# Moving a state-space stage's step-size chain ahead of its convolutions, with a ring of three decay tiles, on one Trainium2 core

## The chip, the cores and the metric

The kernel runs on one core of a Trainium2 chip. The metric is device time in microseconds (us): the median of three runs, lower is better. TensorE (PE) does the matmuls, VectorE (DVE), ScalarE (ACT) and GpSimd (POOL) the elementwise work, SyncE (SP) issues most DMAs and ACT a few. Each engine and each issuing queue takes its instructions in a fixed order; an instruction that waits holds up all that stands behind it.

## The reference, cut to what matters

Two blocks follow each other. The first (a sliding-window attention beside a diagonal state-space layer, then a sparse attention) is untouched. The second computes, for 1024 tokens `h` of width 1024:

```python
proj = h @ w_in                       # xs, z, B, C, dt_raw, glu, cgate
xbc  = silu(conv4(concat(xs, B, C)))  # 4 taps, causal, per channel
dt   = softplus(dt_raw + dt_bias);  a = -exp(a_log)
adt  = dt * a                         # per chunk of 128 tokens:
a_cs = cumsum(adt)                    # running sums of the steps
ldec = exp(a_cs[t] - a_cs[s]), t >= s # "decay" of each head
y_diag = (C B^T * ldec) @ (xs * dt);  state = state * exp(a_cs[-1]) + B^T @ (xs*dt*exp(a_cs[-1]-a_cs))
y_off  = (C @ state) * exp(a_cs)
y_ssm  = rms((y_diag + y_off + d_skip * xs) * silu(z))
u      = glu_a * sigmoid(glu_b);  u = silu(layer_norm(conv31(u)))
y_conf = u * silu(cgate)
out    = concat(y_ssm, y_conf) @ w_out;  h = layer_norm(alpha * h + out)  # then a gated projection
```

## The kernel before, in words

All matmuls of the projections are done in three passes over split operands (a high and a low half, `mm3`, lines 148 to 150). Their weights come in pieces of 128 x 512: SP loads `wraw`, ACT writes the high half `w` (L122), POOL the low half (L123); where `k.wdve` is 2, every second piece is made by VectorE instead (L119, L120). There are 13 slots for pieces and three for raw ones.

The change lies in `phase_c`, the second block. In program order:

1. glu: gated projection, written to `d_u2`.
2. `xbc`: first the 16 columns of `dt_raw`, transposed into `dtt`; then twelve channel tiles of xs, B, C. A tile `xi` (two halves, copied from PSUM by ACT) gets its first tap on VectorE (L1516), three more (L1518), a silu on ACT, and goes to DRAM (`d_xs`, `d_bc`). The tiles `xy` that hold the result have two buffers.
3. the 31-tap convolution of u, eight channel tiles of 31 VectorE passes in PSUM (`cy`, L1258 and L1260), summed over channels in `acc`.
4. `conf_norm`: mean by a matmul over `acc` (`mu`, L1462), subtraction (L1467), squares on ACT (L1469), their sum over channels on POOL (L1471, L1473), variance by matmuls (`var`, L1477), a power on POOL (L168), a spread by matmuls (`rb`, L1482), sixteen multiplications (L1487) and eight silus (L1488).
5. `ssd`: first the step sizes and running sums (L1539 to L1583: some 28 short VectorE passes over 128 x 128, three matmuls, and a row table written to `d_cs`), then eight chunks. A chunk loads `xh`, `bct` and, for each of two groups, a decay tile `ld` of 128 x 8 x 128 (each group has one buffer), which VectorE (L1601), ACT (exp, L1603) and VectorE again (L1614) turn into the matrix of the diagonal product; POOL scales `xh` into `xd` and `xe`; PE does `cb`, `yoff`, `ydiag`, `inc`; VectorE adds up `yS` and the state `st`.
6. cgate: silu of the projection, tile by tile through the staging ring `stg` (three buffers) to `d_cg`; then sixteen tiles `cgl` of it are loaded back (two buffers of their own) and POOL multiplies `cc` by them (L1285).
7. z: the same for z, sixteen tiles of 24 matmuls, through `stg` to `d_z` (L1292, L1293).
8. the out-projection of the convolution half: `msC` (ACT L1307, POOL L1308) times pieces of `w_out`, added to the residual `rC`, written to `d_r`. Its pool stands where the normalized input `hnTC` stood.
9. the out-projection of the state-space half and the last gated projection, which the change leaves as they are.

The program is not run in this order. A scheduler of the language sets each engine's order ahead of time: it gives each engine the instruction that is first in program order among those whose operands and buffers are free in its model, with a lead for weight pieces. A tile from a ring can be written only when the tile that held its buffer before has been read. Before the change that order puts cgate and z (6 and 7) on PE while VectorE is at the convolution (3), and the out-projection (8) among the chunks of `ssd`.

Of the kernel before, what the change touches and what calls it, by code (L numbers as in the profile page):

```python
# [26 lines left out]
WDVE = (0, 0, 0, 2, 2)  # L27
# [1183 lines left out]
def phase_c(k, out, hC):  # L1211
    hnT, sR = hC
    nc, tc, ins = k.nc, k.tc, k.ins
    V, S, G, T = nc.vector, nc.scalar, nc.gpsimd, nc.tensor
    W, Wo = ins["w_in_2"][0], ins["w_out_2"][0]
# [8 lines left out]
    sng = vp.tile([P, 8], F32, name="sng")  # L1224
    stg = sR.enter_context(k.pool("c_stg", side="right"))

    def stage():
        return stg.tile([P, 512], F32, tag="s", name="stg", bufs=3)
    k.wdve = 0
    k.psum(mm=2, tp=1, sd=3, cy=2)  # L1230

# [4 lines left out]
    for j in range(4):  # L1236
        w = [k.wpiece(W, kk, [(2576 + j * 256, 256), (3600 + j * 256, 256)]) for kk in range(KT)]
        for m in range(2):
            ct = 2 * j + m
# [6 lines left out]
                V.scalar_tensor_tensor(sg, pa, cw[:, ct, 34:35], sg, op0=ALU.add, op1=ALU.mult)  # L1246
                nc.sync.dma_start(d_u2[ct * P:(ct + 1) * P, th * 512:th * 512 + 512], sg)
    with ExitStack() as cx:
        xbc(k, cx.enter_context(k.pool("c_xbc")), W, hnT, sw, dtt, d_xs, d_bc)

    acc = up.tile([P, L], F32, name="acc")
    for ct in range(8):
# [12 lines left out]
    sV.close()  # L1265

    sS, (sp,) = stack(k.pool("ssd"))
    ssd(k, sp, dtt, dtx, d_xs, d_bc, d_ys, d_cs)

    for ch in range(2):  # L1270
        w = k.wchunk(W, 4624 + ch * 512, 512)
# [8 lines left out]
    for ct in range(8):  # L1280
        for th in range(2):
            cs = slice(th * 512, th * 512 + 512)
            cg = stg.tile([P, 512], F32, tag="cg", name="cgl", bufs=2)
            nc.sync.dma_start(cg, d_cg[ct * P:(ct + 1) * P, cs])
            G.tensor_tensor(cc[:, ct, cs], cc[:, ct, cs], cg, op=ALU.mult)  # L1285
    for ch in range(2):
# [5 lines left out]
            S.activation(zt, ps, AF.Silu)  # L1292
            nc.scalar.dma_start(d_z[tt * P:(tt + 1) * P, ch * 512:ch * 512 + 512], zt)  # L1293
    sR.close()
    k.wdve = WDVE[4]

    with ExitStack() as co:
        op = co.enter_context(k.pool("c_o", side="right"))
# [189 lines left out]
        S.activation(cc[:, ct], cc[:, ct], AF.Silu, bias=cw[:, ct, 33:34], scale=cw[:, ct, 32:33])  # L1488


def xbc(k, p, W, hnT, sw, dtt, d_xs, d_bc):
    nc = k.nc
    V, S, G, T = nc.vector, nc.scalar, nc.gpsimd, nc.tensor

    w = k.wpack(W, 2560, 16)
    for th in range(2):
        ps = k.mm()
        k.form2(ps[:16], hnT, th * 512, w, KT, 0, 16)
        dr = p.tile([16, 512], F32, tag="dr", name="dr", bufs=1)
        S.activation(dr, ps[:16], AF.Copy)  # L1500
        ps = k.tp()
        for j in range(4):
            T.transpose(ps[:, j * 16:(j + 1) * 16], dr[:, j * P:(j + 1) * P], k.ident[:16, :16])
        S.activation(dtt[:, th * 4:th * 4 + 4].rearrange("p a b -> p (a b)"), ps[:, :64], AF.Copy)
    for ci, c0 in enumerate((2048, 0, 512)):
        w = k.wchunk(W, c0, 512)
        for m in range(4):
            ct = (8, 0, 4)[ci] + m
            xi = p.tile([P, 3 + L], F32, tag="xi", name="xi", bufs=2)
            V.memset(xi[:, 0:3], 0.0)  # L1510
            for th in range(2):
                ps = k.mm()
                k.form2(ps, hnT, th * 512, w, KT, m * P)
                S.activation(xi[:, 3 + th * 512:3 + th * 512 + 512], ps, AF.Copy)
            y = p.tile([P, L], F32, tag="xy", name="xy", bufs=2)
            V.tensor_scalar(y, xi[:, 0:L], sw[:, ct, 0:1], sw[:, ct, 4:5], op0=ALU.mult, op1=ALU.add)  # L1516
            for i in range(1, 4):
                V.scalar_tensor_tensor(y, xi[:, i:i + L], sw[:, ct, i:i + 1], y, op0=ALU.mult, op1=ALU.add)  # L1518
            S.activation(y, y, AF.Silu)
            if ct >= 8:  # L1520
                nc.sync.dma_start(d_bc[(ct - 8) * P:(ct - 7) * P, :], y)
            else:
                xo = p.tile([P, 8, P], F32, tag="xo", name="xo", bufs=2)
                for h in range(2):
                    ps = k.tp()
                    for i in range(4):
                        T.transpose(ps[:, i * P:(i + 1) * P], y[:, (h * 4 + i) * P:(h * 4 + i + 1) * P], k.ident)
                    S.activation(xo[:, h * 4:h * 4 + 4].rearrange("p a b -> p (a b)"), ps, AF.Copy)
                nc.sync.dma_start(d_xs[:, ct * P:(ct + 1) * P].rearrange("(j p) c -> p j c", p=P), xo)


def ssd(k, p, dtt, dtx, d_xs, d_bc, d_ys, d_cs):
    nc, ins = k.nc, k.ins
    V, S, G, T = nc.vector, nc.scalar, nc.gpsimd, nc.tensor
    f = lambda a: a.rearrange("p a b -> p (a b)")

    t = p.tile([P, 4, P], F32, tag="ld0", name="spt", bufs=1)
    a3 = lambda i: t[:, i].rearrange("p (a b) -> p a b", b=16)
    V.tensor_tensor(a3(0), dtt, dtx[:, 0].unsqueeze(1).to_broadcast([P, 8, 16]), op=ALU.add)  # L1539
    V.tensor_scalar(t[:, 1], t[:, 0], -1.0, None, op0=ALU.mult)  # L1540
# [131 lines left out]
```

## Time and profile before

| what | value |
|---|---|
| median of three runs | 2126.88 us (2124.61 to 2127.88) |
| the profiled execution | 2116.4 us, span 2114.6 us |
| busy: PE, DVE, ACT, POOL | 91%, 73%, 38%, 41% of the span |
| POOL L123, low halves of weights | x230, 310.3 us |
| DVE L1260, the 31 taps | x232, 298.7 us, mean 1287 ns |
| granted TensorE clock, mean | 0.96 |

A busy share is an average over stages with different limits. The granted clock is a share of full speed (2.4 GHz; 0.5 is 1.2 GHz). The ends of matmuls are modelled, so a matmul's duration is longer than the distance from its start to the next one's.

### The profile page before, as it was taken

To read this page: it belongs to the slowest core of one execution; us is meant where nothing else is said; L and a number is where in the kernel's file an instruction comes from. 1 tells how busy PE (TensorE), PEld (TensorE's weight loads), DVE (VectorE), ACT (ScalarE), POOL (GpSimd) and SP (SyncE) were. 2 spreads that over 40 slices of the span, in tenths; PEclk is the share of its full clock that TensorE was granted. 3 is DMA by queue.
4 is the path that set the end of the run, shared out by engine and by line. 5 is a ranking of instruction groups with operands and counts; after the bars stand their busy time and mean duration, and the time that the engine had idled before them with its cause. 6 is when DMAs were issued, how large, how long until landed. Compare 5 with 4: busy or idle time off the path is not lost. (4 is left out here: it accounts for less than half of the span.)

```text
span 2114.6 us, 27500 instructions
## 1 busy us (share of the span) xinstructions
PE 1932.8 (91%) x9291; PEld 1565.7 (74%) x9291; DVE 1546.6 (73%) x3051; ACT 813.5 (38%) x1540; POOL 867.9 (41%) x702
## 2 busy tenths in 40 slices
PE   7988889989999898799987999999999659999998
PEld 6777777777888786677865788788888537778786
DVE  8365513674469999698879399899997488957737
ACT  5222327564456885355543121133322411144210
POOL 5566416545322233365545131222232576643204
PEclk9988989999999999899999999999999869999999
DMA  6543332313212212554444132222433445574442
GB/s 199 156 125 94 114 130 83 118 46 110 81 61 70 70 46 79 171 193 140 130 145 173 61 114 71 70 90 90 129 104 101 159 146 169 170 254 165 155 165 100
DMA packets 166694, 256.19 MB, mean 121 GB/s; under 512 B 29078, under 2 KB 77548, under 8 KB 166554
## 3 DMA queue, kind: packets, MB, share of 16 engines
q1 hardware_dynamic: 156330, 236.62, 34.9%
q10 hardware_dynamic: 10224, 17.82, 2.3%
q8 instruction: 73, 1.20, 0.2%
q14 instruction: 67, 0.55, 0.1%
HBM read 185.35 MB, written 75.06 MB: 123 GB/s over the span
## 5 line engine op out<-in xcount | busy, mean ns | idle before, releaser
L123 POOL TENSOR_TENSOR w<-wraw,w 128x512 fp32r<-128x512 f32 (+1 forms) x230 | 310.3, 1365 | 683.4 <-ACT w L122 672.1
L1260 DVE SCALAR_TENSOR_TENSOR cy<-u,cw,cy 128x1024 f32<-128x1024 f32 x232 | 298.7, 1287 | 5.7
L122 ACT ACTIVATE w<-wraw 128x512 fp32r<-128x512 f32 (+1 forms) x230 | 142.0, 622 | 196.2 <-DMA wraw<-in_w_in_dram 53.3
L149 PE MATMUL mm<-hnTC,w 128*128 128x512 f32 (+1 forms) x336 | 131.6, 392 | 0.0
L150 PE MATMUL mm<-hnTC,w 128*128 128x512 f32 (+1 forms) x336 | 131.5, 391 | 0.0
L148 PE MATMUL mm<-hnTC,w 128*128 128x512 f32 (+1 forms) x336 | 131.5, 391 | 0.0
L148 PE MATMUL mm<-w,ms 128*128 128x512 f32 x256 | 103.9, 406 | 8.8 <-ACT ms L1003 7.9
L1149 POOL TENSOR_TENSOR lgB<-lgB,sc 128x1024 f32<-128x1024 f32 (+5 forms) x48 | 84.1, 1780 | 66.9 <-DMA lgB<-d_T 53.4
L150 PE MATMUL mm<-w,ms 128*128 128x512 f32 x256 | 104.6, 409 | 6.3 <-POOL ms L1004 4.1
L1060 ACT ACTIVATE tkj<-sc,tks 128x896 bf16<-128x896 f32 (+2 forms) x93 | 96.3, 1037 | 31.9 <-DVE tks L1056 25.6
L149 PE MATMUL mm<-w,ms 128*128 128x512 f32 x256 | 101.7, 397 | 0.0
L168 POOL TENSOR_TENSOR hr<-hm,mhalf 128x2 f32<-128x2 f32 (+2 forms) x40 | 46.1, 1154 | 115.9 <-DVE hm L398 50.8
L148 PE MATMUL mm<-w,hnTB 128*128 128x512 f32 x192 | 78.0, 407 | 7.2 <-DVE qo L402 7.2
L148 PE MATMUL mm<-w,hnTA 128*128 128x512 f32 (+1 forms) x192 | 73.0, 383 | 8.9 <-DVE qo L402 8.8
L149 PE MATMUL mm<-w,hnTB 128*128 128x512 f32 x192 | 78.0, 407 | 1.8 <-POOL w L123 1.8
L148 PE MATMUL mm<-hnTB,w 128*128 128x512 f32 (+2 forms) x208 | 78.4, 377 | 0.2 <-ACT hnTB L172 0.2
L149 PE MATMUL mm<-hnTB,w 128*128 128x512 f32 (+2 forms) x208 | 78.1, 376 | 0.0
L150 PE MATMUL mm<-hnTB,w 128*128 128x512 f32 (+2 forms) x208 | 78.1, 375 | 0.0
L150 PE MATMUL mm<-w,hnTB 128*128 128x512 f32 x192 | 78.0, 406 | 0.0
L149 PE MATMUL mm<-w,hnTA 128*128 128x512 f32 (+1 forms) x192 | 73.1, 382 | 0.2 <-POOL w L123 0.2
L150 PE MATMUL mm<-w,hnTA 128*128 128x512 f32 (+1 forms) x192 | 73.3, 382 | 0.0
L148 PEld LDWEIGHTS mm<-hnTC,w 128*128 128x128 f32 (+1 forms) x336 | 61.6, 183 | 14.5
(595 smaller groups left out, 5845.6 us busy)
## 6 DMA issues: line engine op xcount, KB each, us to landing
wraw<-in_w_in_dram SPq DMA_DIRECT2D x56, 256.0 KB
wraw<-in_od_w_in_dram SPq DMA_DIRECT2D x48, 256.0 KB
wraw<-in_ev_w_in_dram SPq DMA_DIRECT2D x32, 256.0 KB
wraw<-in_w_in_dram SPq DMA_DIRECT2D x64, 128.0 KB
wraw<-in_w_out_dram SPq DMA_DIRECT2D x32, 256.0 KB
ld<-d_cs SPq DMA_DIRECT2D x16, 512.0 KB
hr<-h SPq DMA_DIRECT2D x24, 256.0 KB
d_T<-d_row SPq DMA_DIRECT2D x8, 576.0 KB
```

The costliest lines, as they stand in the source:

```text
L122: nc.scalar.activation(t[:, 0, :o], raw[:, :o], AF.Copy)
L123: nc.gpsimd.tensor_tensor(t[:, 1, :o], raw[:, :o], t[:, 0, :o].bitcast(F32), op=ALU.subtract)
L148: mm(out, aH, bH, start=start, stop=False)
L149: mm(out, aH, bL, start=False, stop=False)
L150: mm(out, aL, bH, start=False, stop=stop)
L168: self.nc.gpsimd.tensor_tensor(out, ms, self.mhalf[:, :n], op=ALU.pow)
L1060: S.activation(self.junk(n), sc[b], AF.Sign, bias=cand[:, i:i + 1], accum_out=cnt[:, i:i + 1])
L1149: G.tensor_tensor(lg[:, :n], lg[:, :n], self.masks[b], op=ALU.add)
L1260: V.scalar_tensor_tensor(py if i < 30 else y, u[:, i:i + L], cw[:, ct, i:i + 1], py, op0=ALU.mult, op1=ALU.add)
```

## The change

- The chain of step sizes becomes a function `ssd_steps`, called in `xbc` right after `dtt` is there. Its scratch tile takes one of the two `xy` buffers; `tri`, `nacs`, `eac`, `dst`, `cdc` move to the pool `c_vec`.
- The first tap of each `xbc` tile goes from VectorE to ACT.
- The decay tiles of both groups share one ring of three. `xh`, `xd` and `xe` come in halves of 512 columns: three, two and two buffers. The last chunk makes no `xe`.
- The staging ring has four buffers, and the sixteen `cgl` tiles now come from it too, ahead of z's sixteen.
- `k.wdve` is set to 2 only after the first out-projection: its pieces are all made by ACT and POOL.

```diff
@@ phase_c
-    def stage():
-        return stg.tile([P, 512], F32, tag="s", name="stg", bufs=3)
+    def stage(name="stg"):
+        return stg.tile([P, 512], F32, tag="s", name=name, bufs=4)
...
-        xbc(k, cx.enter_context(k.pool("c_xbc")), W, hnT, sw, dtt, d_xs, d_bc)
+        steps = xbc(k, cx.enter_context(k.pool("c_xbc")), vp, W, hnT, sw, dtt, dtx, d_xs, d_bc, d_cs)
...
-    ssd(k, sp, dtt, dtx, d_xs, d_bc, d_ys, d_cs)
+    ssd(k, sp, steps, dtt, dtx, d_xs, d_bc, d_ys, d_cs)
...
-            cg = stg.tile([P, 512], F32, tag="cg", name="cgl", bufs=2)
+            cg = stage("cgl")
...
     sR.close()
-    k.wdve = WDVE[4]
...
     sF.close()
+    k.wdve = WDVE[4]
@@ xbc
-        dr = p.tile([16, 512], F32, tag="dr", name="dr", bufs=1)
+        dr = p.tile([P, 512], F32, tag="xo", name="dr", bufs=2)[:16]
...
+    steps = ssd_steps(k, p, vp, dtt, dtx, d_cs)
     for ci, c0 in enumerate((2048, 0, 512)):
...
-            V.tensor_scalar(y, xi[:, 0:L], sw[:, ct, 0:1], sw[:, ct, 4:5], op0=ALU.mult, op1=ALU.add)
+            S.activation(y, xi[:, 0:L], AF.Identity, scale=sw[:, ct, 0:1], bias=sw[:, ct, 4:5])
@@ ssd_steps (the first part of ssd before)
-    t = p.tile([P, 4, P], F32, tag="ld0", name="spt", bufs=1)
+    t8 = p.tile([P, 8, P], F32, tag="xy", name="spt", bufs=2)
+    t = t8[:, 0:4]
...
-    t1 = p.tile([P, 3, P], F32, tag="ld1", name="spt1", bufs=1)
-    adt, one, ar = t1[:, 0].rearrange("p (a b) -> p a b", b=16), t1[:, 1], t1[:, 2]
+    adt, one, ar = t8[:, 4].rearrange("p (a b) -> p a b", b=16), t8[:, 5], t8[:, 6]
...
-    eac = p.tile([P, 8, 16], F32, name="eac")
+    eac = vp.tile([P, 8, 16], F32, name="eac")
...
     nc.sync.dma_start(d_cs, ar)
+    return tri, nacs, eac, dst, cdc
@@ ssd, in the loop over chunks
-        xh = p.tile([P, D], F32, tag="xh", name="xh", bufs=2)
-        nc.sync.dma_start(xh, d_xs[ts_, :])
+        xhs = []
+        for g in range(2):
+            xhs.append(p.tile([P, 512], F32, tag="xh", name="xh", bufs=3))
+            nc.sync.dma_start(xhs[g], d_xs[ts_, g * 512:(g + 1) * 512])
...
-            ld = p.tile([P, 8, P], F32, tag=f"ld{g}", name="ld", bufs=1)
+            ld = p.tile([P, 8, P], F32, tag="ld", name="ld", bufs=3)
...
-        xd = p.tile([P, D], F32, tag="xd", name="xd", bufs=1)
-        G.tensor_tensor(h3(xd), h3(xh), b64a(dtt, c), op=ALU.mult)
-        xe = p.tile([P, D], F32, tag="xe", name="xe", bufs=1)
-        G.tensor_tensor(h3(xe), h3(xd), b64a(dst, c), op=ALU.mult)
...
+        for g in range(2):
+            xd = p.tile([P, 512], F32, tag="xd", name="xd", bufs=2)
+            G.tensor_tensor(h3(xd), h3(xhs[g]), b64(dtt, g, c), op=ALU.mult)
+            xds.append(xd)
+        for g in range(2 if c < 7 else 0):
+            xe = p.tile([P, 512], F32, tag="xe", name="xe", bufs=2)
+            G.tensor_tensor(h3(xe), h3(xds[g]), b64(dst, g, c), op=ALU.mult)
+            xes.append(xe)
```

The scheduler's order moves with it. PE in `conf_norm`, before (rb spreads the reciprocal deviation; `mm<-w,hnTC` is z):

```order
L149 MATMUL mm<-w,hnTC 128x512
L150 MATMUL mm<-w,hnTC 128x512
L148 MATMUL mm<-w,hnTC 128x512
L1482 MATMUL rb_13528<-ident,rsc 128x128 x4
L1482 MATMUL rb_13529<-ident,rsc 128x128 x4
L149 MATMUL mm<-w,hnTC 128x512
L150 MATMUL mm<-w,hnTC 128x512
```

and now, from the last matmul of z's first two tiles on:

```order
L150 MATMUL mm<-w,hnTC 128x512
L1462 MATMUL mu<-acc,ones 128x512 x2
L1477 MATMUL var<-ones,acc 128x2 x8
L1482 MATMUL rb_13581<-ident,rsc 128x128 x4
L1482 MATMUL rb_13582<-ident,rsc 128x128 x4
L1619 MATMUL cb<-bct 128x128
L1620 MATMUL cb<-ident,bct 128x128
L1619 MATMUL cb<-bct 128x128
L1620 MATMUL cb<-ident,bct 128x128
L1643 MATMUL yoff<-st_13619,bct 128x512
L1648 MATMUL ydiag<-xd,ld 128x64 x8
L1655 MATMUL inc<-xe,bt 128x512
```

Before, all 384 matmuls of z stood ahead of the first chunk. Now 48 do; the next of z come after chunk 0 and the first `yoff` of chunk 1, 280 of them among chunks 1 to 7, and 56 behind the last chunk; the 384 of `msC` follow those.

ACT behind the silus of `conf_norm`, now (before, `L1603 ACTIVATE ld` met no silu of z any more):

```order
L1488 ACTIVATE cc<-cc,cw 128x1024 x8
L1616 ACT_TABLE_LOAD
L1616 ACTIVATE ld<-ld 128x1024
L1625 ACTIVATE bt<-cb 128x256
L1616 ACTIVATE ld<-ld 128x1024 x3
L1292 ACT_TABLE_LOAD
L1292 ACTIVATE stg<-mm 128x512
L1625 ACTIVATE bt<-cb 128x256
L1293 DMA d_z<-stg 128x512
```

The drain of z's first tile stands behind the fourth exp of a decay tile. Exp and silu alternate from here on: 24 table loads, where none stood among the chunks before.

SP at the end of the chunks, now (`bo` and `rC` belong to the out-projection's pool, `wraw` are its pieces):

```order
L1652 DMA d_ys<-yS 128x512 x3
L110 DMA wraw<-in_w_out_dram 128x512 x3
L187 DMA bo<-in_b_out_dram 128x1024
L1309 DMA rC<-d_h_10478 128x1024
L110 DMA wraw<-in_w_out_dram 128x512
L1309 DMA rC<-d_h_10478 128x1024 x2
L110 DMA wraw<-in_w_out_dram 128x512 x2
L1320 DMA d_r<-rC 128x512
L110 DMA wraw<-in_w_out_dram 128x512 x5
```

Five of the sixteen pieces were loaded earlier; of the eleven here eight stand behind the loads `bo` and `rC`, and the last five behind a store of the first result.

## Rows read from the trace of the kernel before

**Rows 1.** Stretches: busy us (instructions) of PE, PEld, DVE, ACT, POOL; granted clock; DMA share, GB/s.
```profile
1675.00:1709.00 34.00, 1.75 (x7) 1.16 (x6) 31.21 (x53) 11.65 (x15) 20.06 (x16) 0.55 0.59 202
1709.00:1731.00 22.00, 12.69 (x46) 9.07 (x46) 12.28 (x12) 5.02 (x8) 16.58 (x10) 0.61 0.54 181
1731.00:1885.00 154.00, 145.50 (x703) 113.44 (x702) 125.98 (x118) 29.80 (x39) 100.00 (x47) 0.98 0.54 177
1885.00:2114.60 229.60, 215.72 (x1010) 176.62 (x1008) 148.04 (x247) 60.69 (x119) 66.76 (x54) 0.99 0.45 158
```
**Rows 2.** Tile mm on PE: duration ns min/median/max, first and last start us, forms.
```profile
L150 PE MATMUL mm<-hnTC,w x336: 387/389/477, 1345.6 to 1582.5; 128*128 128x512 f32 x160, 128*16 128x512 f32 x8
...
L150 PE MATMUL mm<-w,hnTC x128: 388/389/398, 1583.1 to 1674.9; 128*128 128x512 f32 x128
L148 PE MATMUL mm<-w,msC x128: 387/389/799, 1731.3 to 1884.6; 128*128 128x512 f32 x128
```
**Rows 3.** Timeline of PE in z: start, us, line, [idle before <- releaser].
```profile
1605.13 0.39 PE L148 MATMUL mm<-w,hnTC 128*128 128x512 f32 x1
...
1605.81 0.39 PE L148 MATMUL mm<-w,hnTC 128*128 128x512 f32 x1
```
**Rows 4.** Timeline of DVE from the convolution's end to the first chunks.
```profile
1609.43 1.23 DVE L1263 TENSOR_TENSOR acc<-acc,cc 128x1024 f32<-128x1024 f32 x1
1622.51 9.65 DVE L1467 TENSOR_TENSOR cc<-cc,mu 128x512 f32<-128x512 f32 x16 [11.85 <-PE mu L1462]
...
1667.24 9.65 DVE L1487 TENSOR_TENSOR cc<-cc,rb 128x512 f32<-128x512 f32 x16 [7.29 <-PE rb L1482]
...
1709.27 0.29 DVE L1582 COPY spt<-acsT 128x128 f32<-128x128 f32 x1 [0.17 <-PE acsT L1581]
...
1729.25 2.27 DVE L1601 CUSTOM_DVE_ANT_1 ld<-ld,nacs 128x1024 f32<-128x1024 f32 x1 [1.44 <-DMA ld<-d_cs]
```
**Rows 5.** DVE by line, 1340 to 1610: busy us, mean ns | idle before <- releaser.
```profile
L1516 DVE TENSOR_SCALAR xy<-xi,sw 128x1024 f32<-128x1024 f32 x12 | 10.9, 910 | 3.3 <-ACT xi L1514 3.3
```
**Rows 6.** Tile spt (the step chain's scratch): columns as in Rows 2.
```profile
L1549 DVE TENSOR_TENSOR spt<-spt x7: 277/292/1361, 1694.3 to 1702.4; 128x128 f32<-128x128 f32 x7
```
**Rows 7.** Tile sqc (the squares) on ACT and POOL: columns as in Rows 2.
```profile
L1469 ACT ACTIVATE sqc<-cc x8: 1042/1056/1065, 1628.7 to 1650.6; 128x1024 f32<-128x1024 f32 x8
...
L1471 POOL COPY acc<-sqc x1: 1039/1039/1039, 1629.8 to 1629.8; 128x1024 f32<-128x1024 f32 x1
```
**Rows 8.** Timelines of POOL and PE at the variance.
```profile
1640.70 14.82 POOL L1473 TENSOR_TENSOR acc<-acc,sqc 128x1024 f32<-128x1024 f32 x6
1660.02 1.66 POOL L168 TENSOR_TENSOR rsc<-rsc,mhalf 128x8 f32<-128x8 f32 x1 [4.50 <-DVE rsc L1478]
...
1657.90 1.84 PE L1477 MATMUL var<-ones,acc 128*128 128x2 f32 x16
...
1666.08 1.95 PE L1482 MATMUL rb<-ident,rsc 128*128 128x128 f32 x16
```
**Rows 9.** Timeline of ACT: a table load, and a piece that waited for its load.
```profile
1663.64 1.28 ACT L1555 ACT_TABLE_LOAD   x1 [0.39 <-ACT stg L1292]
1664.93 0.21 ACT L1555 ACTIVATE ea<-dtx 128x16 f32<-128x16 f32 x1
...
1688.35 0.63 ACT L122 ACTIVATE w<-wraw 128x512 fp32r<-128x512 f32 x1 [3.82 <-DMA wraw<-in_w_out_dram]
```
**Rows 10.** Timeline of SP: issues of bo, of three pieces, and of a decay tile.
```profile
1675.34 0.33 SPq L187 DMA_DIRECT2D bo<-in_b_out_dram  x1
...
1682.83 1.37 SPq L110 DMA_DIRECT2D wraw<-in_w_out_dram  x3
...
1725.30 0.32 SPq L1600 DMA_DIRECT2D ld<-d_cs  x1
```
**Rows 11.** Tile msC on ACT and POOL: columns as in Rows 2.
```profile
L1307 ACT ACTIVATE msC<-cc x8: 1040/1048/1060, 1726.9 to 1859.8; 128x1024 fp32r<-128x1024 f32 x8
L1308 POOL TENSOR_TENSOR msC<-cc,msC x8: 2355/2652/2852, 1728.1 to 1860.9; 128x1024 fp32r<-128x1024 f32 x8
```

More of the change, by code (lines that the diff above doesn't have):

```diff
@@ L1488, in conf_norm, with xbc @@
         S.activation(cc[:, ct], cc[:, ct], AF.Silu, bias=cw[:, ct, 33:34], scale=cw[:, ct, 32:33])
-def xbc(k, p, W, hnT, sw, dtt, d_xs, d_bc):
+def xbc(k, p, vp, W, hnT, sw, dtt, dtx, d_xs, d_bc, d_cs):
     nc = k.nc
@@ L1529, in xbc, with ssd_steps @@
                 nc.sync.dma_start(d_xs[:, ct * P:(ct + 1) * P].rearrange("(j p) c -> p j c", p=P), xo)
-def ssd(k, p, dtt, dtx, d_xs, d_bc, d_ys, d_cs):
+    return steps
+def ssd_steps(k, p, vp, dtt, dtx, d_cs):
     nc, ins = k.nc, k.ins
@@ L1553, in ssd @@
     V.scalar_tensor_tensor(f(dtt), t[:, 3], 2.0, t[:, 0], op0=ALU.mult, op1=ALU.add)
-    ea = p.tile([P, 16], F32, name="ea")
+    ea = vp.tile([P, 16], F32, name="ea")
     S.activation(ea, dtx[:, 1], AF.Exp)
     V.tensor_scalar(ea, ea, -1.0, None, op0=ALU.mult)
-    t1 = p.tile([P, 3, P], F32, tag="ld1", name="spt1", bufs=1)
-    adt, one, ar = t1[:, 0].rearrange("p (a b) -> p a b", b=16), t1[:, 1], t1[:, 2]
+    adt, one, ar = t8[:, 4].rearrange("p (a b) -> p a b", b=16), t8[:, 5], t8[:, 6]
+    acs = t8[:, 7].rearrange("p (a b) -> p a b", b=16)
     V.tensor_tensor(adt, dtt, ea.unsqueeze(1).to_broadcast([P, 8, 16]), op=ALU.mult)
-    tri = p.tile([P, P], F32, name="tri")
+    tri = vp.tile([P, P], F32, name="tri")
     V.memset(tri, 1.0)
@@ L1563, in ssd @@
     V.memset(one, 1.0)
-    acs = p.tile([P, 8, 16], F32, name="acs")
-    nacs = p.tile([P, 8, 16], F32, name="nacs")
-    eac = p.tile([P, 8, 16], F32, name="eac")
-    dst = p.tile([P, 8, 16], F32, name="dst")
-    cdc = p.tile([P, 8, 16], F32, name="cdc")
+    nacs = vp.tile([P, 8, 16], F32, name="nacs")
+    eac = vp.tile([P, 8, 16], F32, name="eac")
+    dst = vp.tile([P, 8, 16], F32, name="dst")
+    cdc = vp.tile([P, 8, 16], F32, name="cdc")
     ps = k.ps("sd", "acs")
@@ L1583, in ssd @@
     nc.sync.dma_start(d_cs, ar)
+    return tri, nacs, eac, dst, cdc
+def ssd(k, p, steps, dtt, dtx, d_xs, d_bc, d_ys, d_cs):
+    nc, ins = k.nc, k.ins
+    V, S, G, T = nc.vector, nc.scalar, nc.gpsimd, nc.tensor
+    f = lambda a: a.rearrange("p a b -> p (a b)")
+    tri, nacs, eac, dst, cdc = steps
     st = [p.tile([P, 512], F32, name=f"st{g}") for g in range(2)]
@@ L1614, in ssd @@
             V.tensor_tensor(lds[g], lds[g], cb[:, g].unsqueeze(1).to_broadcast([P, 8, P]), op=ALU.mult)
-        xd = p.tile([P, D], F32, tag="xd", name="xd", bufs=1)
-        G.tensor_tensor(h3(xd), h3(xh), b64a(dtt, c), op=ALU.mult)
-        xe = p.tile([P, D], F32, tag="xe", name="xe", bufs=1)
-        G.tensor_tensor(h3(xe), h3(xd), b64a(dst, c), op=ALU.mult)
-        G.tensor_tensor(h3(xh), h3(xh), dtx[:, 2].unsqueeze(2).to_broadcast([P, 16, 64]), op=ALU.mult)
+        xds, xes = [], []
+        for g in range(2):
[6 more added lines that the diff above has]
+            xes.append(xe)
+        for g in range(2):
+            G.tensor_tensor(h3(xhs[g]), h3(xhs[g]), dtx[:, 2, g * 8:g * 8 + 8].unsqueeze(2).to_broadcast([P, 8, 64]),
+                            op=ALU.mult)
         for g in range(2):
@@ L1627, in ssd @@
             for h in range(8):
-                T.matmul(pd[:, h * 64:(h + 1) * 64], lds[g][:, h], xd[:, g * 512 + h * 64:g * 512 + (h + 1) * 64],
+                T.matmul(pd[:, h * 64:(h + 1) * 64], lds[g][:, h], xds[g][:, h * 64:(h + 1) * 64],
                          start=True, stop=True)
             V.tensor_tensor(y, pd, y, op=ALU.add)
-            G.tensor_tensor(y, y, xh[:, gs], op=ALU.add)
+            G.tensor_tensor(y, y, xhs[g], op=ALU.add)
             nc.sync.dma_start(d_ys[ts_, gs], y)
@@ L1634, in ssd @@
                 pi = k.ps("sd", "inc")
-                T.matmul(pi, bt[:, g], xe[:, gs], start=True, stop=True)
+                T.matmul(pi, bt[:, g], xes[g], start=True, stop=True)
                 V.tensor_tensor(h3(st[g]), h3(st[g]), b64(cdc, g, c), op=ALU.mult)
```

## The prediction

> **What bounds the kernel now.** I read the table of stretches first, then the matmul groups on PE, then the timelines around the point where PE stops. Up to the end of z PE is without a gap: the projections through cgate end at 1582.5 us, z at 1675 [rows 2]. Then comes a hole: in 1675 to 1709 PE is busy for 1.75 of 34 us, in 1709 to 1731 for 12.69 of 22, at a granted clock of 0.55 and 0.61 [rows 1]. From 1731 the out-projection of the convolution half runs among the chunks; PE is busy for 145.5 of 154 us and ends it at 1885.4 [rows 1, 2]. The last stage keeps PE busy for 215.7 of 229.6 us [rows 1]. So after the hole the bound is PE, and what the change can win is PE's idle time: 32 + 9 + 8.5 = about 50 us between 1675 and 1885. VectorE sets when the hole ends: it does the step chain after the last multiplication by rb, from 1676.9 to 1709.6 [rows 4].
>
> **The change part by part.** I follow PE, and ask when its queue, in the order shown for the change, reaches the last matmul of the out-projection. What stands before cgate's end is not counted: PE's matmuls there are the same, and PE now has time to spare at its end.
>
> *The convolution's end.* VectorE is the bound now up to 1610.7, the end of the last sum in acc [rows 4]. Off it go the twelve first taps, 10.9 us and up to 3.3 us of waiting before them [rows 5]; ACT has room for twelve passes of about 1.06 us [rows 7]. On it come the 28 passes of the step chain: 8 us at the median of 0.29 us, and 15 us if a quarter of them take the longest, 1.36 us [rows 6]. I take 11, since most of them lie at the median. The scratch tile holds one of two xy buffers meanwhile, so the first four tiles of xbc must each wait for the store of the one before; a couple of us of VectorE's order may be lost on that. Sum: 1610.7, with -6 to +8. The three matmuls and the DMA to d_cs move along and hide behind the taps.
>
> *conf_norm.* Before, z stood in front of mu, var and rb in PE's queue: VectorE waited 11.85 us for mu, and rb began 4.4 us after the power was done [rows 4, 8]. Now only the chain itself is left. Handing a matmul to VectorE took 1.16 us (rb at 1666.08, multiplication at 1667.24 [rows 4, 8]): 1611.9. The first two of sixteen subtractions 1.2, a square 1.06, POOL's copy 1.04 [rows 4, 7]: 1615.2. Seven sums at 14.82 / 6 = 2.47 [rows 8]: 1632.5. Variance 1.84, power 1.66, rb and its handing on 1.2, the sixteen multiplications 9.65 [rows 4, 8]: 1646.9. PE has stood still here, so I add 3 us for matmuls at half clock, the level that the hole of before shows [rows 1]: 1650, against 1676.9 before. So 27 us are won here for VectorE, and the 33 us of the step chain on top: the first chunk starts at 1650 instead of 1710.
>
> *The hole.* PE pays for both. Ahead of mu its queue now holds only 48 matmuls of z. Three of them take 0.68 us [rows 3], so they end 1582.5 + 10.9 = 1593.4, and then PE waits for VectorE: mu, var, rb and chunk 0 stand in front of the rest of z. Two things make that order: z's tiles take staging buffers behind the sixteen cgl tiles, which POOL reads only after conf_norm, and two PSUM buffers hold two tiles. From the end of the step chain to the first matmul of the next projection chunk 0 took 1731.3 - 1709.6 = 22 us [rows 2, 4]; I take it unchanged. It saves a wait for the decay table, but VectorE now does a third decay tile in it (2.27 us), and z's first drain on ACT stands behind the fourth exp, whose tile is loaded only when the first is free (3.95 us from issue to use [rows 4, 10]). So 17 to 26 us, and z goes on at 1672.
>
> *z among the chunks.* Left are 336 matmuls of z, 76.2 us [rows 3]. Chunks 1 to 7 cost PE 145.5 - 384 x 0.227 = 58.4 us in 1731 to 1885 [rows 1, 3], of which 2 are done ahead of z. With the 8.5 us of gaps of that stretch: 141 us, to 1813. VectorE has 126 us of work in that stretch [rows 1], a part of it the residual, which now goes after the chunks, so PE is the bound. For the gaps 0 to 18 us are the bounds. The ring of three, the halves of xh, xd, xe and the two that are not made save waits of VectorE and POOL that stand beside a busier PE: nothing for the end, and only the gaps if that cover were thinner.
>
> *Into the out-projection.* msC's pool stands where the input of z stood: bo was issued at 1675.34, right at z's end [rows 2, 10]. In the new order the fourth of eleven pieces is loaded behind bo and rC, and ACT makes that piece and z's last drain before the first msC. Issues 1.3 us, the load 1688.35 - 1682.83 = 5.5 us [rows 9, 10], ACT 0.6 + 0.6 + 1.05, POOL's low half 2.65 [rows 11] of which the first passes cover some: 10 us without matmuls. Then the last five pieces wait behind the first store of a result, which needs the first half tile (5.4 us): about 7 us more in the second half tile. Sum 17 (bounds 5 and 25: loads that land in 2 us, or twice as slow). That VectorE no longer makes such pieces takes work from it that was hidden, and puts it on ACT and POOL, where it is part of these 17.
>
> *Sum.* 1813 + 17 + 87.1 = 1917 for the end of the out-projection, against 1885.4: 32 us later. The last stage starts from the same state, so I leave its 229.6 us. On the profiled execution (2116.4) that is 2148; the median of the runs shown lies 10.5 us higher, so the forecast is 2126.9 + 32 = **2159 us**. All bounds on the good side (-6, -3, -5, -8.5, -12) give no change, all on the bad side (+8, +4, +10, +8) 2189.
>
> *A rule and a row.* A switch of ACT's function tables costs 1.28 us in this trace, and the next activation follows at once: load at 1663.64, exp at 1664.93 [rows 9]. Four switches in a chunk are then 5.1 us, and ACT does about 9 of 20 us (two exps of 1.06, two drains of 0.6, the copy of bt, the switches). The Trainium skill (ScalarE: Activation LUTs, What ACT_TABLE_LOAD costs) gives 1283 ns for the load, which the row bears out, and a drain of some 1380 ns on top, which it does not show. By that page's figures I estimate 14 us of ACT in a chunk, which is still no bound, so the sum would stay.
>
> **The rivals.**
> *The table switches pace the chunks (chance 0.12).* ACT's order alternates drains of z with exps, so each drain, and with it the PSUM buffer of the next tile but one, waits for a switch, and each exp for a drain. If all 24 lie on PE's path, 24 x 1.28 = 31 us: 2190 us. For it: two PSUM buffers only, and a fixed order. Against: a tile of z is 5.4 us of PE work, and a drain with its switch under 2. The same page of the Trainium skill (Rules for kernel authors) says to group functions by table set, which speaks against this order; at its 2.66 us I estimate 64 us in place of the 31.
> *Small loss (0.07).* Pieces land ahead of need and chunk 0 takes 17: 2142 us.
> *No change (0.06).* All the good bounds together, 2127.
> *Faster (0.06).* The chunks set the pace by VectorE, and PE's 58 us in them are mostly waiting: the ends of matmuls are modelled, so a busy row can hide it. Then z fits into gaps that were there anyway. It decides at 109 us for chunks 1 to 7 with z in place of 141, the point where 32 us are gone; VectorE's own work there is 126 us less the residual and the tail of chunk 0. At 100 us the run takes 2159 - 41 = 2118 us. For it: VectorE's first decay passes took 2.27 us [rows 4], and a ring of three starts them earlier. Against: z's 76 us leave only 33 for seven chunks, under 5 us each, where the rows show 8.3.
> *Forecast (0.69),* with a range of its own from 2145 to 2176.
>
> **How the numbers follow.** A median of this kernel can tell about 0.2% (4 us) from no change. Slower by more: forecast, switches and small loss, 0.88. Same 0.06, faster 0.06. The range is 2138 to 2190: it leaves out the faster and the unchanged case and a part of the switches.
>
> **What would show it.** Right: PE without work but for 48 matmuls of z between about 1583 and 1610, mu within 2 us of acc's end, VectorE's first decay tile near 1650, z going on near 1672, a stretch of only msC matmuls of about 104 us, its end near 1917. The step chain wrong: its passes mostly over 1 us. Wrong altogether: z going on before 1640, chunks 1 to 7 in under 109 us, or an out-projection that ends before 1885.

## The result, and the profile after

The changed kernel takes 2138.5 us (median of four runs, 2137.1 to 2140.0) against 2126.9: slower, at a ratio of 1.006 (95% interval 1.0045 to 1.0075). One further execution of the kernel before took 6893 us and is left out. The forecast was slower too, but by 32 us; about 12 came. The profiled execution (2137.6 us, span 2135.9) is 21.3 us of span behind that of before, and 8 of these are there at the start of cgate's last matmul already (1590.6 us instead of 1582.5). Six of the 8 have nothing to do with the change: the first block, which it leaves as it is, already does its last matmul `mm<-w,ms` 6.3 us later. (Tile mm on PE, before and after, columns as in [rows 2].)

```profile
L150 PE MATMUL mm<-w,ms x256: 387/389/628, 384.0 to 1149.3; 128*128 128x512 f32 x128
L150 PE MATMUL mm<-w,ms x256: 387/392/687, 385.1 to 1155.6; 128*128 128x512 f32 x128
```

Over the profiles of all kernels below but e2 and e6, which are slower there, the start of cgate's last matmul lies anywhere from 1580.1 to 1590.6, and the kernel before itself took 2113.6 to 2128.5 us in later runs. So kernels are compared by places counted **from the start of cgate's last matmul** (the lines shown have the times of their own profile), and by ratios to the kernel before, run beside each kernel.

Stretches of the changed kernel (columns as in [rows 1]), cut at the last sum of the convolution, the last multiplication by rb, z's going on, z's end and the out-projection's end:

```profile
1590.80:1614.40 23.60, 11.02 (x49) 8.81 (x47) 22.99 (x18) 3.65 (x6) 6.49 (x5) 0.78 0.78 255
1614.40:1658.60 44.20, 12.21 (x42) 9.33 (x42) 19.44 (x33) 12.45 (x12) 27.91 (x18) 0.58 0.01 3
1658.60:1681.00 22.40, 12.97 (x47) 8.40 (x48) 18.11 (x19) 11.90 (x12) 22.40 (x14) 0.62 0.58 182
1681.00:1815.20 134.20, 130.48 (x648) 102.20 (x646) 85.38 (x86) 59.10 (x67) 101.53 (x69) 0.99 0.49 160
1815.20:1909.20 94.00, 90.40 (x386) 74.24 (x387) 26.14 (x30) 22.87 (x35) 37.80 (x20) 0.96 0.54 190
1909.20:2135.90 226.70, 215.08 (x1008) 176.47 (x1006) 147.06 (x247) 58.94 (x113) 65.73 (x52) 0.99 0.45 155
```

The hole of before (56 us wide, [rows 1]) has become one of 90: in it PE has 48 matmuls of z and the small work of conf_norm and chunk 0, 36 us in all, much of it at the lower clock (0.58, 0.62). In return the chunks run beside z, where PE stands for 3.7 us only, and the out-projection runs bare. The same in the tile mm on PE (columns as in [rows 2]): z's 128 groups of three matmuls are now spread to 1814.3, and msC starts behind them.

```profile
L150 PE MATMUL mm<-hnTC,w x336: 387/389/481, 1353.2 to 1590.6; 128*128 128x512 f32 x160, 128*16 128x512 f32 x8
...
L148 PE MATMUL mm<-w,hnTC x128: 387/389/799, 1590.8 to 1814.3; 128*128 128x512 f32 x128
```

The timelines of PE, DVE and ACT in the hole answer to [rows 4, 8]: mu comes with the last sum instead of behind z, the multiplications start at 1649 instead of 1667 (58.4 instead of 84.7 us after cgate's last matmul), yet PE waits for each step of it.

```profile
1614.44 3.57 PE L1462 MATMUL mu<-acc,ones 128*128 128x512 f32 x4 [12.62 <-DVE acc L1263]
1641.24 3.57 PE L1477 MATMUL var<-ones,acc 128*128 128x2 f32 x16 [23.22 <-POOL acc L1473]
...
1616.55 9.66 DVE L1467 TENSOR_TENSOR cc<-cc,mu 128x512 f32<-128x512 f32 x16 [2.17 <-PE mu L1462]
...
1648.98 9.66 DVE L1487 TENSOR_TENSOR cc<-cc,rb 128x512 f32<-128x512 f32 x16 [3.97 <-PE rb L1482]
...
1622.06 2.00 ACT L1469 ACTIVATE sqc<-cc 128x1024 f32<-128x1024 f32 x2 [22.64 <-DVE cc L1467]
```

VectorE's waits from xbc to the last sum, 1353 to 1614.5 (us in total, times, longest), answer to [rows 5]:

```profile
DVE xy L1519 <- ACT xy L1517: 4.4, 3, 2.2
DVE spt L1543 <- ACT dtt L1504: 1.2, 1, 1.2
```

The way into the out-projection, by timelines of SP, ACT, PE and DVE, by the tile wraw on ACT, and by stretches:

```profile
1734.25 0.33 SPq L110 DMA_DIRECT2D wraw<-in_w_out_dram  x1
1743.13 3.27 SPq L110 DMA_DIRECT2D wraw<-in_w_out_dram  x3
1747.88 0.33 SPq L110 DMA_DIRECT2D wraw<-in_w_out_dram  x1
1751.35 5.55 SPq L110 DMA_DIRECT2D wraw<-in_w_out_dram  x2
1758.78 0.33 SPq L110 DMA_DIRECT2D wraw<-in_w_out_dram  x1
...
1812.48 2.82 SPq L110 DMA_DIRECT2D wraw<-in_w_out_dram  x3
1815.39 0.38 SPq L187 DMA_DIRECT2D bo<-in_b_out_dram  x1
...
1829.23 7.19 SPq L110 DMA_DIRECT2D wraw<-in_w_out_dram  x5
...
1810.44 0.63 ACT L122 ACTIVATE w<-wraw 128x512 fp32r<-128x512 f32 x1
...
1811.12 1.31 ACT L122 ACTIVATE w<-wraw 128x512 fp32r<-128x512 f32 x2
1815.43 0.63 ACT L122 ACTIVATE w<-wraw 128x512 fp32r<-128x512 f32 x1 [3.00 <-DMA wraw<-in_w_out_dram]
...
L115 ACT ACTIVATE w<-wraw,sng x16: 707/723/726, 1893.6 to 1927.6; 128x512 fp32r<-128x512 f32 x16
...
1817.55 0.50 PE L148 MATMUL mm<-w,msC 128*128 128x512 f32 x1 [2.38 <-ACT msC L1306]
...
1819.99 0.80 PE L150 MATMUL mm<-w,msC 128*128 128x512 f32 x1 [1.26 <-POOL msC L1307]
...
1828.08 0.69 DVE L1319 TENSOR_TENSOR rC<-mm,rC 128x512 f32<-128x512 f32 x1
...
1836.69 0.69 DVE L1319 TENSOR_TENSOR rC<-mm,rC 128x512 f32<-128x512 f32 x1 [5.84 <-PE mm L150]
1838.51 0.69 DVE L1319 TENSOR_TENSOR rC<-mm,rC 128x512 f32<-128x512 f32 x1 [1.12 <-PE mm L150]
...
1820.00:1826.00 6.00, 6.00 (x14) 4.74 (x15) 1.67 (x2) 0.63 (x1) 6.00 (x4) 0.51 0.98 378
1826.00:1836.00 10.00, 10.00 (x45) 8.25 (x44) 4.84 (x3) 2.49 (x4) 6.97 (x5) 1.00 0.47 148
```

PE stands for 2.38 + 1.26 us, then runs at half clock until 1826, and has no gap from 1820 on. The second half tile ends 8.6 us after the first (5.4 would be its own work) and the third only 1.8 us later: the order mixes the second half of tile 0 with the first half of tile 1. By 1759 SP has issued eight of the sixteen pieces, not five; ACT splits the last three of these eight only from 1810.44 on. Of the five loads behind the first store (1829.23) only two are pieces of this projection. The other three are the first of the last stage, whose pieces are split at L115.

### The profile page after: what moved, and what is told of

It reads as the page before. It is cut to its first block, busy times and chain, and to the rows that moved or that the text cites. A ratio compares the mean times of both kernels' runs of the same rounds, so it can differ in the third digit from the quotient of the medians.

```text
span 2135.9 us, 27582 instructions
## 1 busy us (share of the span) xinstructions
PE 1940.5 (91%) x9291; PEld 1572.1 (74%) x9291; DVE 1501.1 (70%) x3023; ACT 862.8 (40%) x1584; POOL 891.5 (42%) x732
## 4 chain that ended last, share of the span: by engine, by line
PE 48%; DVE 23%; issue 12%; DMA 7%; POOL 5%; ACT 3%; SPq 1%; DVEq 0%; POOLq 0%; ACTq 0%
PE mm L150 9%; PE mm L148 9%; PE mm L149 9%; DVE cy L1260 4%; DVE tkj L1062 2%; POOL w L123 2%; DMA wraw<-in_w_in_dram 2%; PE pg L148 1%; PE pg L150 1%; PE pg L149 1%; PE ydiag L1648 1%; PE tph L181 1%; PE ix L898 1%; DVE tks L1064 1%; DVE lgB L1162 1%
## 5 line engine op out<-in xcount | busy, mean ns | idle before, releaser
L123 POOL TENSOR_TENSOR w<-wraw,w 128x512 fp32r<-128x512 f32 (+1 forms) x238 | 325.6, 1383 | 645.9 <-ACT w L122 643.2
L122 ACT ACTIVATE w<-wraw 128x512 fp32r<-128x512 f32 (+1 forms) x238 | 146.6, 623 | 200.0 <-DMA wraw<-in_w_in_dram 54.4
L149 PE MATMUL mm<-hnTC,w 128*128 128x512 f32 (+1 forms) x336 | 131.5, 391 | 0.0
L149 PE MATMUL mm<-w,ms 128*128 128x512 f32 x256 | 101.3, 396 | 0.0
L149 PE MATMUL mm<-w,hnTB 128*128 128x512 f32 x192 | 78.6, 410 | 1.8 <-POOL w L123 1.8
L149 PE MATMUL mm<-hnTB,w 128*128 128x512 f32 (+2 forms) x208 | 78.1, 376 | 0.0
L149 PE MATMUL mm<-w,hnTA 128*128 128x512 f32 (+1 forms) x192 | 73.1, 381 | 0.4 <-POOL w L123 0.4
```

Source lines behind the costliest of these rows:

```text
L122: nc.scalar.activation(t[:, 0, :o], raw[:, :o], AF.Copy)
L123: nc.gpsimd.tensor_tensor(t[:, 1, :o], raw[:, :o], t[:, 0, :o].bitcast(F32), op=ALU.subtract)
L149: mm(out, aH, bL, start=False, stop=False)
```

## The experiments

All twelve, counted from cgate's last matmul: the last sum in acc, the last multiplication by rb, z's last matmul but one (at L149; the last starts 0.2 us later), the first and last of msC (starts of instructions, us).

| kernel | acc | rb | z | msC first | msC last | ratio to before (95%) |
|---|---|---|---|---|---|---|
| before | 26.9 | 93.7 | 92.2 | 148.8 | 302.5 | 1 |
| changed | 22.6 | 67.4 | 224.0 | 226.9 | 318.2 | 1.0060 (1.0045 to 1.0075) |
| e1 own ring | 22.8 | 95.6 | 92.2 | 171.4 | 294.5 | 0.9950 (0.9933 to 0.9967) |
| e2 taps on VectorE | 26.2 | 71.0 | 224.5 | 227.4 | 319.0 | 1.0123 (1.0104 to 1.0141) |
| e3 pieces on VectorE | 22.8 | 67.6 | 224.8 | 227.1 | 316.9 | 1.0060 (1.0045 to 1.0075) |
| e4 decay tiles | 22.8 | 67.6 | 223.7 | 226.7 | 317.1 | 1.0061 (1.0044 to 1.0078) |
| e5 half of z | 22.9 | 91.2 | 174.0 | 181.0 | 304.2 | 0.9987 (0.9976 to 0.9998) |
| e6 steps alone | 26.1 | 93.3 | 92.2 | 166.9 | 301.1 | 1.0022 (1.0008 to 1.0035) |
| e7 ring alone | 26.8 | 71.6 | 226.9 | 233.8 | 333.2 | 1.0135 (1.0113 to 1.0157) |
| e8 own ring, cgl on VectorE | 22.8 | 95.5 | 92.2 | 158.8 | 286.6 | 0.9908 (0.9883 to 0.9933) |
| e9 taps alone | 20.3 | 91.2 | 92.2 | 145.3 | 301.7 | 0.9985 (0.9969 to 1.0000) |
| e10 z copied | 22.8 | 67.6 | 220.8 | 223.4 | 314.2 | 1.0050 (1.0031 to 1.0069) |
| e11 chunk body of before | 22.7 | 67.5 | 221.3 | 224.0 | 315.3 | 1.0047 (1.0030 to 1.0064) |
| e12 lean | 22.8 | 94.2 | 93.4 | 155.6 | 297.1 | 0.9969 (0.9953 to 0.9984) |

### e1: cgl in its own ring

```diff
-        return stg.tile([P, 512], F32, tag="s", name=name, bufs=4)
+        return stg.tile([P, 512], F32, tag="s", name="stg", bufs=3)
...
-            cg = stage("cgl")
+            cg = stg.tile([P, 512], F32, tag="cg", name="cgl", bufs=2)
...
-            xe = p.tile([P, 512], F32, tag="xe", name="xe", bufs=2)
+            xe = p.tile([P, 512], F32, tag="xe", name="xe", bufs=1)
```

> The changed kernel, but cgl has a ring of its own again (two tiles, three for the other staging; xe gets one buffer instead of two, to make room). Ring theory (z behind cgl is what costs, the rest of the change gains): the order puts 154 z matmuls of three ahead of var's end as before, all of z ahead of chunk 0, and the first four chunks bare. z ends near 1680 us instead of 1815, the multiplications by rb near 1685, chunks 0 to 3 bare until about 1746, the out-projection ends near 1868 instead of 1909: 2096 us, between 2088 and 2115. Rival (the loss sits in the fewer VectorE pieces, the taps on ACT or the table switches): at most the switches go, 2137 with 4 us either way.

Faster than both kernels: 0.995, 1.1% (23 us) under the changed one. rb comes where expected (95.6; 1685 was 94.4); the bare chunks take longer, they were to end at 155 (1746) and msC starts at 171.4. Stretches (as in [rows 1]): all of z without a gap, the bare chunks, the chunks with msC.

```profile
1583.30:1675.50 92.20, 92.20 (x420) 76.27 (x419) 38.82 (x46) 27.17 (x41) 39.59 (x26) 1.00 0.36 114
1675.50:1754.70 79.20, 46.04 (x166) 31.18 (x164) 59.74 (x58) 26.63 (x32) 79.20 (x52) 0.64 0.64 210
1754.70:1877.80 123.10, 123.10 (x586) 98.38 (x587) 79.22 (x82) 25.66 (x36) 78.33 (x48) 0.98 0.51 178
```

In the second POOL is busy throughout; e8 starts from that.

### e2: first taps on VectorE again

```diff
-            S.activation(y, xi[:, 0:L], AF.Identity, scale=sw[:, ct, 0:1], bias=sw[:, ct, 4:5])
+            V.tensor_scalar(y, xi[:, 0:L], sw[:, ct, 0:1], sw[:, ct, 4:5], op0=ALU.mult, op1=ALU.add)
```

> The changed kernel, but the twelve first taps of xbc are VectorE's again. If VectorE's load alone sets the convolution's end, as the prediction had it, the end of acc moves 11 us later (twelve passes of 0.91 us) and everything behind it with it, PE standing still meanwhile: 2149 us. Rival: VectorE has slack inside the stretch (it waits for xbc tiles anyway), the end of acc moves under 4 us: 2138 to 2142.

0.6% (13 us) slower than the changed kernel: the size of the theory, but not its place. The convolution ends 3.6 us later, of which 0.8 is left at msC's end; the stretch from the first matmul of xbc to cgate's last grows from 237 to 247 us. PE's waits in that stretch, of which neither the kernel before nor the changed one has any, are 5.4 us, with slower matmuls behind them (up to 777 ns, against 497):

```profile
PE tp L1528 <- ACT xy L1520: 3.1, 1, 3.1
PE mm L148 <- ACT xi L1515: 2.3, 1, 2.3
```

### e3: every second piece on VectorE again

```diff
     sR.close()
+    k.wdve = WDVE[4]
...
     sF.close()
-    k.wdve = WDVE[4]
```

> The changed kernel, but every second piece of the out-projection of the convolution half is VectorE's again. If the pieces on ACT and POOL make the way into the out-projection longer, they come earlier: the first msC matmul 1 to 3 us earlier and the stretch to its end shorter, 2134 to 2136 us. Rival: the pieces are limited by their loads and by the raw buffers, and who splits them makes no difference: 2138 with 2 us either way.

Same ratio, out-projection 1.3 us earlier: the rival. Who splits the pieces is worth nothing here.

### e4: one decay tile for each group

```diff
-            ld = p.tile([P, 8, P], F32, tag="ld", name="ld", bufs=3)
+            ld = p.tile([P, 8, P], F32, tag=f"ld{g}", name="ld", bufs=1)
```

> The changed kernel, but with one decay tile for each group of heads instead of a ring of three. If the ring is what keeps PE full among the chunks (3.7 us of idle time where the prediction had 8.5), z among the chunks takes 4 to 15 us longer: 2142 to 2153 us. Rival: z's matmuls cover the chunks' waits anyway and only chunk 0 counts, which loses its third decay pass ahead of the first product (2.3 us): 2136 to 2139 us.

Same ratio, z's end at 223.7: the rival. Beside z the ring of three is worth nothing.

### e5: half of z ahead of cgl

```diff
+    zhalf(0)
     for ct in range(8):
         for th in range(2):
             cg = stage("cgl")
...
-    for ch in range(2):
+    zhalf(1)
```

> The changed kernel with z cut in two: the first eight token tiles of z (192 matmuls) stand in the program ahead of the cgl loop, the other eight behind it. Ring theory: 154 z matmuls of three go ahead of mu, 86 more ahead of var's end, and 144 stay for the chunks. Counted from cgate's end: z's first part ends at 54.5 us, mu at 36 (behind 154 of them, as in the run with a ring of its own), the multiplications end at about 78 against 67.4 in the changed kernel, the rest of z goes on at about 100, and 33 + 87 + 54 us of matmuls and some 11 of gaps and slow clock behind it end the out-projection at about 285, against 318 in the changed kernel and 302.5 before: ratio 0.991 to the kernel before, between 0.985 and 0.996. Rival (PE's hole isn't what costs; VectorE and POOL pace the chunks whatever PE has to do among them): no gain from moving z, the out-projection ends at 318 plus the 10 us by which mu comes later, ratio 1.01.

0.9987: 0.7% under the changed kernel, not the 1.5% expected. The place of z is again worth time, but rb ends at 91 instead of 78. Timeline of ACT:

```profile
1640.90 0.63 ACT L122 ACTIVATE w<-wraw 128x512 fp32r<-128x512 f32 x1 [6.89 <-DMA wraw<-in_w_out_dram]
1642.06 1.28 ACT L122 ACTIVATE w<-wraw 128x512 fp32r<-128x512 f32 x2 [0.53 <-DMA wraw<-in_w_out_dram]
1643.25 1.04 ACT L1472 ACTIVATE sqc<-cc 128x1024 f32<-128x1024 f32 x1
```

Pieces of the out-projection now stand in ACT's queue ahead of the fourth square, and wait 6.9 us for their load; the sums, var and rb wait with them.

### e6: the step chain alone

```diff
-    ssd(k, sp, dtt, dtx, d_xs, d_bc, d_ys, d_cs)
+    ssd(k, sp, steps, dtt, dtx, d_xs, d_bc, d_ys, d_cs)
...
+    steps = ssd_steps(k, p, vp, dtt, dtx, d_cs)
...
```

> The kernel before with only the early step chain (the tiles that the chunks read moved to the long-lived pool; taps, pieces, staging rings and chunk buffers as before). If the early chain is the gaining part: the order puts all of z ahead of chunk 0 and three bare chunks behind it; VectorE carries chain and taps, so xbc on PE takes some 9 us longer as in the run with taps on VectorE, and counted from cgate's end the multiplications end at about 90, bare chunks at 18.5 us each take it to 147, and the out-projection ends at about 279 against 302.5 before: 14 us faster, ratio 0.9935, between 0.988 and 1.0. Rival (the hole behind z only changes its name, from step chain to bare chunks, and the taps' 10 us come on top): 1.0 to 1.006.

1.0022, the rival. xbc on PE takes 9.7 us longer, as in e2, and behind z the bare chunks last from 93 to 167: the chain of 33 us went, the hole stayed.

### e7: the shared ring alone

```diff
-        return stg.tile([P, 512], F32, tag="s", name="stg", bufs=3)
+        return stg.tile([P, 512], F32, tag="s", name=name, bufs=4)
...
-            cg = stg.tile([P, 512], F32, tag="cg", name="cgl", bufs=2)
+            cg = stage("cgl")
```

> The kernel before with only the shared staging ring of four (cgl takes its tiles from it). Ring theory: 48 z matmuls stay ahead of mu, then PE waits for conf_norm and for most of the step chain (19 z matmuls go in it, 50 in chunk 0). Counted from cgate's end: the multiplications end at 72 us, the chain at 105, chunk 0 at 127; 267 z matmuls (61 us), 58 us of chunks, 4 of gaps, 7 of transition and 87 of out-projection end at about 344 against 302.5: 41 us slower, ratio 1.0195, between 1.013 and 1.026. Rival (the order of z makes no difference): 1.0 with 0.002 either way.

1.0135: 29 us slower, the largest loss of all, where 41 were expected (msC's end 333 instead of 344). PE's waits in its hole are the steps of conf_norm and the step chain:

```profile
PE acs L1570 <- DVE spt L1559: 28.5, 1, 28.5
PE var L1477 <- POOL acc L1473: 23.0, 1, 23.0
PE mu L1462 <- DVE acc L1263: 16.8, 1, 16.8
```

### e8: own ring, and cgl's multiplications on VectorE

On top of e1's edits:

```diff
-            G.tensor_tensor(cc[:, ct, cs], cc[:, ct, cs], cg, op=ALU.mult)
+            V.tensor_tensor(cc[:, ct, cs], cc[:, ct, cs], cg, op=ALU.mult)
```

> The changed kernel with cgl in a ring of its own, as in the first run, and the sixteen multiplications by cgl on VectorE. POOL theory (in the bare chunks of the first run POOL is busy for 76 of 76 us while PE waits, so POOL sets when msC can begin): 16 times 1.33 us leave POOL, some 12 us come on VectorE, which was busy for 56 of those 76 us; the order lets msC in one chunk earlier. The first msC matmul comes 15 to 20 us earlier than 171 us after cgate's end, the out-projection ends near 278 against 294.5: ratio 0.988 to the kernel before, between 0.984 and 0.992. Rival (the chain of decay table, exp and products over VectorE and ACT paces the bare chunks, and VectorE gets longer): 0.995 or above.

0.9908, the fastest kernel here, 1.5% under the changed one. msC starts 12.6 us earlier than in e1, less than the 15 to 20 expected. The bare chunks:

```profile
1672.30:1738.90 66.60, 36.03 (x124) 22.96 (x122) 58.87 (x64) 25.46 (x30) 44.68 (x32) 0.63 0.64 220
```

POOL is down to 45 of 67 us, and now VectorE is nearly full with 59. A multiplication takes 0.77 us there (median) against 1.49 on POOL in e1. The Trainium skill (Trainium Architecture — The Big Picture, The five engines, in one table) calls POOL twice as slow as VectorE in streaming elementwise work; the trace agrees.

### e9: the taps alone

> The kernel before with only the twelve first taps on ACT. Queue theory (in the kernel before conf_norm stands in PE's queue behind z, so an earlier end of the convolution is worth only what the order moves up): mu goes behind 140 z matmuls of three instead of 171, var behind 313 instead of 324, so the multiplications end some 2.5 us earlier, and all behind them: ratio 0.9988, between 0.997 and 1.0005. Rival (VectorE's load is worth its full time: 10.9 us): 0.995.

The edit is e2's in the other direction, on the kernel before. 0.9985: the queue theory. The last sum comes 6.6 us earlier, rb 2.5, msC's end 0.8.

### e10: z drained as a copy

```diff
-            S.activation(zt, ps, AF.Silu)
+            S.activation(zt, ps, AF.Copy)
```

> The changed kernel with z drained as a plain copy: silu of z is left out of the computation, the order of PE and VectorE stays word for word, and 23 table loads of 1.28 us go from ACT, since a copy needs no other table than exp does. Forecast (the switches stand beside a busy PE): z's first drain comes 1.3 us earlier, nothing else changes, 2136 to 2138.5 us where the changed kernel takes 2138.5, ratio to the kernel before between 1.004 and 1.0075. Rival of the prediction (the switches pace the chunks): up to 23 x 1.28 = 29 us go, ratio 0.993.

1.0050, which can't be told from 1.0060; z ends 3.2 us earlier. So the rival on table switches is out. In the changed kernel these loads lie between z's going on and its end (ACT by line: busy us, mean ns | idle before):

```profile
L1616 ACT ACT_TABLE_LOAD x11 | 14.1, 1283 | 6.2 <-DVE ld L1614 3.7 <-ACT stg L1292 2.4
L1292 ACT ACT_TABLE_LOAD x11 | 14.1, 1283 | 4.7 <-PE mm L150 4.6
```

28 us of loads, of which 3 at most were on the path.

### e11: the chunk's buffers of before

```diff
-            xhs.append(p.tile([P, 512], F32, tag="xh", name="xh", bufs=3))
+        xh = p.tile([P, D], F32, tag="xh", name="xh", bufs=2)
...
-            ld = p.tile([P, 8, P], F32, tag="ld", name="ld", bufs=3)
+            ld = p.tile([P, 8, P], F32, tag=f"ld{g}", name="ld", bufs=1)
```

> The changed kernel with the chunk's buffers as before: one decay tile for each group, whole xh, xd and xe, all eight xe made. If the halves and the ring are what took the gaps among z from the 8.5 us expected to 4.3, the stretch from z's going on to its end gets 4 to 6 us longer, and chunk 0 up to 3 more: the out-projection ends 4 to 9 us later than 318 after cgate's end, ratio 1.008 to 1.0105. Rival (z stands ready in PE's order, so the chunks' waits are covered whoever makes them): within 2 us, ratio 1.005 to 1.007.

Close to the rival, and past it: 1.0047, z's end 2.7 us earlier, where the theory wanted 4 to 9 us more. Halves and ring together are worth nothing beside z.

### e12: the gaining parts alone

> The kernel before with the early step chain, the taps on ACT and the multiplications by cgl on VectorE, and nothing else of the change: staging rings, pieces and chunk buffers as before. If the shared ring is the only part that costs, and the chunk buffers and the pieces are worth nothing either way, this does what the changed kernel with cgl in its own ring and on VectorE did (0.9908), and up to 4 us better, since the order lets msC in half a chunk earlier: the out-projection ends between 283 and 287 after cgate's end, ratio 0.987 to 0.992. Rival (whole tiles and one decay tile for each group make the bare chunks longer, since PE has nothing else there): the out-projection ends at 290 to 296, ratio 0.993 to 0.997.

The edits are those of e6, e9 and e8, on the kernel before. 0.9969 and an end at 297.1: the rival by its ratio, 1 us past the end that it gave. Beside bare chunks the buffers (or the pieces, which differ too; not separated) do count. PE, in the bare chunks and behind them:

```profile
1680.20:1742.40 62.20, 29.41 (x104) 17.75 (x102) 58.49 (x68) 19.11 (x23) 28.53 (x16) 0.62 0.66 218
1742.40:1883.90 141.50, 138.03 (x648) 109.64 (x649) 97.66 (x96) 28.92 (x40) 79.18 (x39) 0.95 0.50 173
```

PE does 29 us of work in the hole, against 36 in e8, and stands 3.5 us later on, where e8 has no gap.

## Why the prediction was wrong in size

Right was the mechanism: z behind cgl in one ring costs PE a hole that the early step chain doesn't pay back. e7 shows it alone (+1.35%), e1 takes it out (-1.1%). By the prediction's own steps, from cgate's end:

- *Convolution's end*: 28.2 forecast, 23.8 measured. The taps (-10.9) and the chain (+11) were to cancel. By e9 the taps alone move the last sum by 6.6 us; in the changed kernel, where the chain comes on top, it stands only 2.3 us later than in e9 (22.6 against 20.3). VectorE's waits for ACT did not go, they grew from 3.3 [rows 5] to 5.6 us.
- *conf_norm*: 39.3 forecast, 44.2 measured. The first square was to wait for two subtractions; the order makes all eight of mu's first half before the second half's, so it waits for nine (1616.55 to 1622.06 above). The rows [rows 4, 7] show the same in the kernel before (1622.51 to 1628.7). The multiplications end at 68.0, forecast 67.5; that this fits is luck, since the two misses cancel.
- *The hole*: chunk 0 as forecast, z goes on at 91.1 instead of 89.5.
- *z among the chunks* was put at 141 us and took 133.5 (1681.7 to 1815.2). The 8.5 us of gaps were carried over from [rows 1]; 3.7 came, and PE's work was 130.5 us instead of 132.6. By e4 and e11 the new buffers are not the reason for the smaller gaps; that z always stands ready in PE's order is likely, but only argued.
- **The step that failed most is "Into the out-projection", 17 us: it took 6.9** (94.0 less 87.1). Its first term, 10 us of standing, was 3.6. The piece that ACT makes ahead of the first msC is the fourth of the eleven that it still has to split (1810.44, two at 1811.12, 1815.43), but the prediction took it for the fourth load in SP's list, behind bo and rC. It is the first load there: issued at 1812.48, before z ended, and landed within 3 us, not 5.5. So next to nothing of the issue and the load was left when z ended at 1815.2; ACT's piece, drain and first msC stayed (2.38 us), and 1.26 of POOL's 2.65. The second term, 7 us behind the first store, was 0: only two of the five pieces there belong to this projection, and between the ends of the first and the second half tile PE had 40 matmuls to do instead of 24 (8.6 us). Against that, half clock until 1826 cost about 3 us (the rest of the 6.9), which the sum did not have.
- *The last stage*: 226.7 us instead of 229.2 is no effect; over all profiles it lies from 227 to 232.

Together: -4.4 + 4.9 + 1.1 - 7.5 - 10.1 = -16, so 16 us instead of 32 to the out-projection's end, and 12 to 13 by the medians. Rivals: table switches out (e10), "faster" out (z and chunks 1 to 7 took 133 us, not 109). "Small loss" had half of the case, pieces that land ahead of need (chunk 0 took 23 us, not its 17); its 0.07 was too low, since the mixed half tiles stood in the order already.

## What to carry to other kernels

A ring of buffers shared by two loops also fixes their order: what stands behind a late reader in the ring stands behind everything that reader waits for, here 90 us of PE. Before costing a stall at a hand-over, follow each load in the issuing queue to the instruction that uses it, and look in the order for what else the engine has to do then: here a load counted as late was already under way, and a half tile of the next token tile hid the rest. Work moved off a busy engine pays only where that engine's chain is the last wait: the same twelve taps were worth 0.6% beside the step chain and 0.15% without it.

## What was not expected of the hardware

A pause of 3.6 us (with two pairs of matmuls in it) brought TensorE's granted clock from 0.99 in the stretch before to about 0.5, its lower level, and it stayed there until 1826, though PE worked without a gap from 1820: 14 matmuls took 6.0 us instead of 3.2, so the pause cost nearly as much again as it lasted. The last matmul of the unchanged first block starts anywhere from 1146.7 to 1157.0 us over the fourteen profiles, which come from several chips, and 6 us apart in three from one chip (e5 to e7): nearly as much as the whole effect.
